# A decoder layer's mixer: one Gelu operation behind the attention's turned rows in place of a gelu in pieces

## The chip, the cores and the metric

The kernel runs on one core of a Trainium2 chip. The metric is the device time of one execution in microseconds. Five engines work side by side, each through its own instructions in order: TensorE (PE in the profile, its weight loads PEld), VectorE (DVE), ScalarE (ACT), GpSimd (POOL) and SyncE (SP), which issues most DMAs. They wait for each other on semaphores.

## The reference

One layer of a decoder trunk on 512 tokens of width 1024: a half-step SwiGLU FFN, a mixer, and a second half-step FFN, each with an RMS norm before and after it. The change lies in the mixer:

```python
proj = h @ w_in                       # split into x_lru, gate_lru, q, k, v
xc = causal_depthwise_conv(x_lru, conv_w, conv_b)
r, i = sigmoid(block_diag(xc, w_rg, b_rg)), sigmoid(block_diag(xc, w_ig, b_ig))
log_a = 8 * r * log_sigmoid(lam)
a, u = exp(log_a), sqrt(-expm1(2 * log_a)) * (i * xc)
h_t = a_t * h_(t-1) + u_t             # a scan over the tokens
y_lru = h * gelu(gate_lru)            # gelu in its tanh form
y_attn = sliding_window_sink_attention(q, k, v, sinks)
y = concat(rms_norm(y_lru, g_lru_out), rms_norm(y_attn, g_attn_out)) @ w_o
```

The recurrence has 512 channels, the attention 8 heads of 64 with a window of 128 tokens.

## The kernel before

Everything is float32, and a product is made of three TensorE products of split operands (`mm3`, L502 to L507: high by high, high by low, low by high), into one of eight PSUM banks of 128x512. The author writes the order of every engine by hand: the instructions stand in an engine's queue in the order in which the Python code makes them, and the framework adds the waits.

In the mixer the 512 channels are four chunks `ci` of 128 channels by 512 tokens. Before the attention loop, the convolution, the sigmoid gates, q, k and v are made. The attention loop (L1724 to L1755) runs over eight units `now`, a unit being a block `b` of 128 query tokens and one of two key heads `n`, plus two rounds to drain. In a round:

- `scores` (L1624): VectorE folds the two key blocks into one, takes the maximum and the exponent's offset; ahead of the first unit of a block TensorE makes the score products (L1622).
- `pump` (L1569): TensorE does some steps of the gate's product (`gt`, the four chunks of `gate_lru`), as filling.
- `turn_p` (L1661): TensorE turns the last unit's exponentials (`pt`, L1666), ScalarE copies them out (L1668), and POOL makes the two masked versions `pp` and `pa` (L1672, L1673).
- `exps` (L1651): ScalarE's exponentials of this unit (L1656).
- `run_due` (L1527): the steps set down for this round with `later`: pieces of the gelu, and the decay of the recurrence (`decay_a`, `decay_b`, L1574 to L1582).
- `values` (L1676): TensorE multiplies the masked exponentials of the unit before the last with the values (`po`, L1688 and L1689), VectorE divides (L1691 to L1696) into the row block `yn`; `b` below 2 lives in the tile `home`.

Beside this stand in the loop the roots of the recurrence (L1585, at `now == 5`, between two loads of ScalarE's function tables), `root_u` (L1588, at 6: chunks 0 and 1 on POOL, 2 and 3 on VectorE), and the scans (L1593: 2 and 3 at `now == 7`, 0 after the eighth unit, 1 after the loop). `W.fill` and `deferred` split the weights of the output product into high (ScalarE, L209) and low parts (VectorE, L185 and L214).

The gelu is in pieces. `gelu_a` scales the gate by the norm's factor (VectorE, L1427) and squares it (ScalarE, L536); `gelu_b` makes the cubic (VectorE, L1541); `gelu_c` takes the Tanh (ScalarE, L1544); `gelu_d` makes (1 + tanh) times gate (VectorE, L1548). Chunks 0 and 1 go through all of it in the loop, one piece a round. For chunks 2 and 3 the Tanh comes after the loop, and POOL and VectorE multiply the recurrence in two steps (L1797 with the gate, L1794 with 1 + tanh). POOL does the first multiplication of all four chunks. The factor of a half is left out, and the statistics' epsilon is four times as large (`eps4`, L1803).

After the loop `root_rms` and `invert_rms` (L1708, L1711) take the root of the mean squares of the row blocks `yns` and scale them: blocks 0 and 1 on ScalarE (L1715), 2 and 3 on VectorE (L1717). TensorE turns them (`atp`, L1770), ScalarE writes the high parts (`x_high`, L580), VectorE the low parts (`x_low`, L583), and the output product begins with the attention's half (`wo_attn`, L1813 and L1816). Then the recurrence's squares are summed (`add_square`, L1789 and L1791), TensorE makes the statistics (`rms_lru`, L550), VectorE scales the recurrence (L1833), and its half of the output product follows.

Of the kernel before, what the change touches and what calls it, by code (L numbers as in the profile page):

```python
# [11 lines left out]
AF = mybir.ActivationFunctionType  # L12
ALU = mybir.AluOpType
# [4 lines left out]
NB = T // P  # L18
# [5 lines left out]
KC = C // P  # L24
# [97 lines left out]
def tile_layer(ctx: ExitStack, tc: tile.TileContext, out: bass.AP, **ins: bass.AP):  # L122
    nc = tc.nc
    pe, dve, act, pool, sync = nc.tensor, nc.vector, nc.scalar, nc.gpsimd, nc.sync
# [11 lines left out]
    ALL = slice(0, T)  # L136
# [25 lines left out]
    def wt(name, w=T, dt=F32):  # L162
        return tmp.tile([P, w], dt, tag="w", name=name, bufs=NW)
# [311 lines left out]
    mean_c = filled("mean_c", 1, 1.0 / C)  # L475
    eps = filled("eps", 1, EPS)
    eps4 = filled("eps4", 1, 4 * EPS)
    dummy = const.tile([P, 1], F32, name="dummy")

    def preload(func):  # L480
        act.activation(dummy, eps, func)
# [52 lines left out]
    def square(src, sl, name, scale=1.0):  # L534
        sq = wt(f"sq_{name}")[:, sl]
        act.activation(sq, src, AF.Square, scale=scale)  # L536
        return sq
# [44 lines left out]
    def x_low(x, src, gain, sl):  # L582
        dve.scalar_tensor_tensor(x[1][:, sl], src, gain, x[0].bitcast(F32)[:, sl], op0=ALU.mult, op1=ALU.subtract)  # L583
# [612 lines left out]
    tps = turn_early()  # L1196
# [48 lines left out]
    tps = {c: turn(1, c) for c in range(0, KD, 2)}  # L1245
# [115 lines left out]
    for g, (f0, f1) in enumerate(GROUPS1):  # L1361
# [18 lines left out]
        for c in range(KD):  # L1380
# [25 lines left out]
            b = pair_banks[c] if c < 2 else product(W.take(), xs, name=f"ya{g}{c}")  # L1406
# [97 lines left out]
    for j in range(4):  # L1504
        b = in_product(f"pq{j}")
# [10 lines left out]
    preload(AF.Exp)  # L1516


    GC, GA = 0.7978845608028654, 0.044715
    Gs = {}  # L1520

    todo = []
# [1 line left out]
    def later(i, fn, *args):  # L1524
        todo.append((i, fn, args))

    def run_due(i):  # L1527
        nonlocal todo
        due, todo = [t for t in todo if t[0] <= i], [t for t in todo if t[0] > i]
        for _, fn, args in due:  # L1530
            fn(*args)


    gts, gqs = {}, {}

    def gelu_a(ci, b):
        gts[ci] = scaled(wt(f"gt{ci}"), b)
        gqs[ci] = square(gts[ci], ALL, f"g{ci}", (GC * GA) ** 0.5)

    def gelu_b(ci):  # L1540
        dve.scalar_tensor_tensor(gqs[ci], gqs[ci], GC, gts[ci], op0=ALU.add, op1=ALU.mult)  # L1541

    def gelu_c(ci):
        act.activation(gqs[ci], gqs[ci], AF.Tanh)  # L1544

    def gelu_d(ci):
        G = t2k(f"G{ci}")
        dve.scalar_tensor_tensor(G, gqs[ci], 1.0, gts[ci], op0=ALU.add, op1=ALU.mult)  # L1548
        Gs[ci] = G

    def fill_steps():
        for ci in range(KC):
            w = W.take(2)
            b = bank(f"gt{ci}")
            for k in range(KD):
                mm3(b, w, k, mx.xs[k], k == 0, k == KD - 1)
                if k < KD - 1:
                    yield
            if ci < KC - 1:
                for d, fn in enumerate((gelu_a, gelu_b, gelu_c, gelu_d)[:4 if ci < 2 else 1]):  # L1560
                    later(now + d, fn, *((ci, b) if d == 0 else (ci,)))
            else:
                gts[ci] = b
            yield

    now = 0
    steps = fill_steps()

    def pump(n):  # L1569
        for _ in range(n):  # L1570
            next(steps, None)


    def decay_a(ci):  # L1574
# [3 lines left out]
        m = gqs["m", ci] = wt(f"m{ci}")  # L1578
        act.activation(m, a, AF.Square)

    def decay_b(ci):
        dve.scalar_tensor_tensor(th[ci], gqs["m", ci], 1.0, th[ci], op0=ALU.add, op1=ALU.mult)  # L1582

    def root(ci):
        act.activation(th[ci], th[ci], AF.Sqrt)  # L1585

    def root_u(ci):
        (pool if ci < 2 else dve).tensor_mul(us_[ci], us_[ci], th[ci])  # L1588

    hl = us_  # L1590

    def scan(ci):
        dve.tensor_tensor_scan(hl[ci], rs_[ci], us_[ci], initial=0.0, op0=ALU.mult, op1=ALU.add)  # L1593


    scale = HD ** -0.5
    yns = []
# [108 lines left out]
    rat = const.tile([P, NB], F32, name="rat")  # L1706
# [3 lines left out]

    def invert_rms(bs):  # L1711
        dve.reciprocal(rat[:, bs], rat[:, bs])
        for b in range(NB)[bs]:
            if b < 2:
                act.activation(yns[b], yns[b], AF.Copy, scale=rat[:, b:b + 1])  # L1715
            else:
                dve.tensor_scalar(yns[b], yns[b], rat[:, b:b + 1], None, op0=ALU.mult)  # L1717

    units = [(b, n) for b in range(NB) for n in range(2)]
    for ci in range(KC):  # L1720
# [2 lines left out]
    n_units = len(units)  # L1723
    for now in range(n_units + 2):  # L1724
        if now < n_units:
            scores(*units[now])
            if now == 7:
                for ci in (2, 3):
                    scan(ci)
            if now in FILLS:  # L1730
                W.fill(FILLS[now])
        pump(PUMPS[now][0])
        if 0 <= now - 1 < n_units:
            turn_p(*units[now - 1])
        if now < n_units:
            exps(*units[now])
        if now == 0:
            deferred.run()
        if now <= n_units:
            run_due(now - 1)  # L1740
        pump(PUMPS[now][1])
        if 0 <= now - 2:
            values(*units[now - 2])
        if now == 5:
            for ci in range(KC):
                root(ci)
            preload(AF.Exp)
        if now == 6:
            for ci in range(KC):
                root_u(ci)  # L1750
        if now == n_units:
            scan(0)
            deferred.run()
            preload(AF.Sqrt)
            root_rms(slice(0, NB - 1))  # L1755


    root_rms(slice(NB - 1, NB))
    invert_rms(slice(0, NB - 1))
    invert_rms(slice(NB - 1, NB))  # L1760
    pump(100)
    ysp = [None] * KD
    scan(1)
    run_due(n_units + 1)
    gelu_b(KC - 2)
    gts[KC - 1] = scaled(wt(f"gt{KC - 1}"), gts[KC - 1])
    tps = [bank(f"atp{ci}") for ci in range(KC)]
    for ci, tp in enumerate(tps):
        for b in range(NB):
            pe.transpose(tp[:, b * P:(b + 1) * P], yns[b][:, ci * P:(ci + 1) * P], ident)  # L1770
        ysp[ci + KC] = (spare.pop(), spare.pop()) if spare else (t2k(f"yah{ci}", F32R), t2k(f"yal{ci}", F32R))
        x_high(ysp[ci + KC], tp, col("g_attn_out", ci), ALL)
        if ci == 2:
            gqs[KC - 1] = square(gts[KC - 1], ALL, f"g{KC - 1}", (GC * GA) ** 0.5)
            for i in (0, 1):
                x_low(ysp[i + KC], tps[i], col("g_attn_out", i), ALL)
            gelu_b(KC - 1)
            preload(AF.Exp)
    for ci in (2, 3):
        gelu_c(ci)  # L1780
    for ci in (2, 3):
        x_low(ysp[ci + KC], tps[ci], col("g_attn_out", ci), ALL)


    accl = tmp.tile([P, T], F32, tag="acc", name="acc_lru", bufs=3)
# [4 lines left out]
        else:  # L1790
            dve.tensor_add(accl, accl, square(hl[ci], ALL, f"l{ci}"))  # L1791

    def gated(ci):
        dve.scalar_tensor_tensor(hl[ci], gqs[ci], 1.0, hl[ci], op0=ALU.add, op1=ALU.mult)  # L1794

    for ci in (0, 2, 1, 3):
        pool.tensor_mul(hl[ci], hl[ci], Gs[ci] if ci in Gs else gts[ci])  # L1797
    for ci in (2, 3):
        gated(ci)
    for ci in range(KC):  # L1800
        add_square(ci)
    preload(AF.Sqrt)
    lrms = [InvRms([accl], mean_c, h, f"lru{h}", eps4) for h in range(2)]  # L1803

    res = Residual("r2", lambda c: col("mix_post_g", c))
    EARLY = KD - LATE
# [236 lines left out]
```

## Time and profile before

| | |
|---|---|
| time, three runs | 846.61, 846.87, 849.55 us; median 846.87 |
| the profiled execution | 846.56 us, its span 844.9 us |
| TensorE's granted clock | 0.998 |
| busy, of the span | TensorE 99%, VectorE 87%, ScalarE 62%, POOL 23% |
| convolution, gates, q, k, v | about 380 to 408 us |
| attention loop | about 408 to 456 us |
| turned rows, output product | from 457 us |

Times in a row of a timeline are the start from the beginning of the span and the length, both in us; then come engine, line of the kernel, operation, tiles written and read, shape and type, and a count of rows merged. Brackets at the end give idle time ahead of the row and what ended it. Rows of one engine overlap, since an engine begins the next operation before the last is done; what one operation holds of an engine is therefore read from start to start.

### The profile page before, as it was taken

To read this page: it belongs to the slowest core of one execution; us is meant where nothing else is said; L and a number is where in the kernel's file an instruction comes from. 1 tells how busy PE (TensorE), PEld (TensorE's weight loads), DVE (VectorE), ACT (ScalarE), POOL (GpSimd) and SP (SyncE) were. 2 spreads that over 40 slices of the span, in tenths; PEclk is the share of its full clock that TensorE was granted. 3 is DMA by queue.
4 is the path that set the end of the run, shared out by engine and by line. 5 is a ranking of instruction groups with operands and counts; after the bars stand their busy time and mean duration, and the time that the engine had idled before them with its cause. 6 is when DMAs were issued, how large, how long until landed. Compare 5 with 4: busy or idle time off the path is not lost.

```text
span 844.9 us, 12588 instructions
## 1 busy us (share of the span) xinstructions
PE 834.7 (99%) x4568; PEld 722.2 (85%) x4568; DVE 733.5 (87%) x1032; ACT 523.3 (62%) x842; POOL 196.2 (23%) x203
## 2 busy tenths in 40 slices
PE   9999999999999999999999999999999999999997
PEld 8988888988988998997787899888888888888886
DVE  4978999998979865889889679799998998998996
ACT  6646856666666654466787456436657767666562
POOL 2023000140320333334526055212004114032001
PEclk9999999999999999999999999999999999999999
DMA  7249419397595899222511131158539939769742
GB/s 251 77 130 347 157 54 319 85 248 255 133 249 180 172 274 331 71 89 84 161 43 50 50 101 51 50 118 269 194 118 225 314 96 251 259 144 252 306 145 100
DMA packets 123614, 143.74 MB, mean 170 GB/s; under 512 B 23896, under 2 KB 81568, under 8 KB 123040
## 3 DMA queue, kind: packets, MB, share of 16 engines
q1 hardware_dynamic: 109232, 111.86, 41.4%
q0 software_dynamic: 14176, 30.94, 17.0%
q8 instruction: 36, 0.59, 0.3%
q14 instruction: 26, 0.21, 0.1%
q10 hardware_dynamic: 144, 0.13, 0.0%
HBM read 100.45 MB, written 40.89 MB: 167 GB/s over the span
## 4 chain that ended last, share of the span: by engine, by line
PE 92%; DVE 4%; ACT 2%; issue 1%; DMA 1%; SPq 0%; DVEq 0%; ACTq 0%
PE aa L955 10%; PE ab L955 10%; PE da L955 5%; PE db L955 5%; PE yaa L1346 3%; PE bb L955 3%; PE ba L955 3%; PE yda L1346 2%; PE ya L506 2%; PE ya L505 2%; PE ya L507 2%; PE aa L885 1%; PE a_first L1205 1%; PE yab L1883 1%; PE yab L1884 1%; PE yab L1882 1%
## 5 line engine op out<-in xcount | busy, mean ns | idle before, releaser
L1115 POOL DMA_DIRECT2D yp_a<-stage x42 | 36.8, 1066 | 180.7 <-ACT stage L1112 163.5
L1115 POOL DMA_DIRECT2D yp_b<-stage x42 | 36.4, 1057 | 143.7 <-ACT stage L1112 121.4
L505 PE MATMUL ya<-hha,whi_ad 128*128 128x512 f32 x62 | 24.1, 389 | 0.0
L506 PE MATMUL ya<-hla,whi_ad 128*128 128x512 f32 x62 | 24.1, 389 | 0.0
L507 PE MATMUL ya<-hha,wlo_ad 128*128 128x512 f32 x62 | 24.1, 389 | 0.0
L688 POOL TENSOR_TENSOR acca_r<-acca_r,sq_r 128x512 f32<-128x512 f32 x6 | 8.1, 1358 | 51.9 <-ACT sq_r L536 51.9
L2001 POOL TENSOR_TENSOR last<-yp,grow 128x512 f32<-128x512 f32 x3 | 3.9, 1294 | 58.5 <-DVE yp L1991 58.5
L524 PE MATMUL an<-xh_mx,whi_xl 128*128 128x256 f32 x64 | 15.8, 287 | 0.0
L525 PE MATMUL an<-xh_mx,wlo_xl 128*128 128x256 f32 x64 | 15.5, 283 | 0.0
L1998 ACT ACTIVATE ysq<-yp 128x512 f32<-128x512 f32 (+1 forms) x8 | 4.8, 606 | 16.2 <-DVE yp L1991 16.2
L505 PE MATMUL gt<-xh_mx,whi_gt 128*128 128x512 f32 x32 | 14.2, 444 | 0.0
L507 PEld LDWEIGHTS ya<-hha,wlo_ad 128*128 128x128 f32 x62 | 11.6, 188 | 2.4
L505 PEld LDWEIGHTS ya<-hha,whi_ad 128*128 128x128 f32 x62 | 11.6, 188 | 2.4
L506 PEld LDWEIGHTS ya<-hla,whi_ad 128*128 128x128 f32 x62 | 11.6, 188 | 2.4
L1112 ACT COPY stage<-yab 128x512 f32<-128x512 f32 x12 | 6.5, 605 | 10.9 <-DMA yp_b<-stage 7.3
L536 ACT ACTIVATE sq_r<-yp_a 128x256 f32<-128x256 f32 (+1 forms) x10 | 5.0, 503 | 12.9 <-DVE yp_a L678 5.9
L505 PE MATMUL pq<-xh_mx,whi_q 128*128 128x512 f32 x32 | 12.8, 400 | 0.0
L505 PE MATMUL pub<-xh_f,whi_bu 128*128 128x512 f32 x32 | 12.6, 395 | 0.0
L507 PE MATMUL gt<-xh_mx,wlo_gt 128*128 128x512 f32 x32 | 12.6, 394 | 0.0
L505 PE MATMUL pgb<-xh_f,whi_bg 128*128 128x512 f32 x32 | 12.6, 393 | 0.0
L506 PE MATMUL gt<-xl_mx,whi_gt 128*128 128x512 f32 x32 | 12.6, 392 | 0.0
L506 PE MATMUL pq<-xl_mx,whi_q 128*128 128x512 f32 x32 | 12.5, 390 | 0.0
(2022 smaller groups left out, 3520.3 us busy)
## 6 DMA issues: line engine op xcount, KB each, us to landing
yp_a<-stage POOLq DMA_DIRECT2D x50, 256.0 KB, 8.8
yp_b<-stage POOLq DMA_DIRECT2D x50, 256.0 KB, 9.4
h_a<-za SPq DMA_DIRECT2D x16, 256.0 KB
hxa<-h_a SPq DMA_DIRECT2D x16, 256.0 KB
h_b<-zb SPq DMA_DIRECT2D x16, 256.0 KB
hxb<-h_b SPq DMA_DIRECT2D x16, 256.0 KB
xn<-in_x SPq DMA_DIRECT2D x8, 256.0 KB
xT_hbm<-xT POOLq DMA_DIRECT2D x2, 1024.0 KB, 9.3
```

Of the source, the lines that this page charges most:

```text
L505: pe.matmul(ps, hi[:, k, :], xh, start=start, stop=False)
L506: pe.matmul(ps, hi[:, k, :], xl, start=False, stop=False)
L507: pe.matmul(ps, lo[:, k, :], xh, start=False, stop=stop)
L524: pe.matmul(ps[:, sl], hi[:, k, :], xh, start=k == 0, stop=False)
L525: pe.matmul(ps[:, sl], lo[:, k, :], xh, start=False, stop=False)
L885: pe.matmul(o, w[:, k, js], x, start=first and i + j + k == 0, stop=k == 3 and i == 2, skip_group_check=True)
L955: pe.matmul(b[tb], x[:, blk], w[:, k, :], start=first and q + k + j == 0, stop=q + k == 2 and j == 2, skip_group_check=True)
L1115: pool.dma_start(o, st.rearrange("p (a b) -> p a b", a=2) if len(o.shape) == 3 else st, accum_op=ALU.add)
L1205: pe.matmul(banks[j][:, HALF[0]], ws[j][part][:, k, :], n1.xs[k][xpart][:, HALF[0]], start=k == 0 and part == xpart, stop=stop and k == KD ...
L1346: pe.matmul(o, a[:, k, ms], x[:, js], start=first and i + k + m % 2 == 0, stop=k == 1 and i == 2, skip_group_check=True)
L1882: pe.matmul(banks[i], hh[:, js], hi[:, k, :], start=first and k == 0, stop=False, skip_group_check=True)
L1883: pe.matmul(banks[i], hh[:, js], lo[:, k, :], start=False, stop=False, skip_group_check=True)
```

## The change

The gelu becomes one ScalarE operation, `Gelu_apprx_tanh`, over the scaled gate, in place. All four chunks of the gate are only scaled in the loop (chunk 3 after it), into tiles of their own. The four Gelus stand on ScalarE behind the four high parts of the turned rows, after a load of their table. The squares, the cubics, the Tanhs, the last products and `eps4` go. VectorE makes all products of the recurrence: all four `root_u`, chunks 0 and 1 one round later than before, and after the low parts the four products with the Gelu. POOL keeps only the masks there. The normalised rows are scaled in another order: in the last round of the loop, ahead of its `values`, the reciprocal of blocks 0 to 2 is taken and ScalarE scales block 0; after the loop VectorE scales blocks 2, 1 and then 3. Scan 1 stands behind the scaling of gate 3.

```diff
-    def gelu_a(ci, b):
-        gts[ci] = scaled(wt(f"gt{ci}"), b)
-        gqs[ci] = square(gts[ci], ALL, f"g{ci}", (GC * GA) ** 0.5)
...
-    def gelu_d(ci):
-        G = t2k(f"G{ci}")
-        dve.scalar_tensor_tensor(G, gqs[ci], 1.0, gts[ci], op0=ALU.add, op1=ALU.mult)
-        Gs[ci] = G
+    def turned_gate(ci, b):
+        Gs[ci] = scaled(t2k(f"G{ci}"), b)
+
+    def gelu(ci):
+        act.activation(Gs[ci], Gs[ci], AF.Gelu_apprx_tanh)
...
-            if ci < KC - 1:
-                for d, fn in enumerate((gelu_a, gelu_b, gelu_c, gelu_d)[:4 if ci < 2 else 1]):
-                    later(now + d, fn, *((ci, b) if d == 0 else (ci,)))
-            else:
-                gts[ci] = b
+            later(now, turned_gate, ci, b)
...
     def root_u(ci):
-        (pool if ci < 2 else dve).tensor_mul(us_[ci], us_[ci], th[ci])
+        dve.tensor_mul(us_[ci], us_[ci], th[ci])
...
     def invert_rms(bs):
         dve.reciprocal(rat[:, bs], rat[:, bs])
-        for b in range(NB)[bs]:
-            if b < 2:
-                act.activation(yns[b], yns[b], AF.Copy, scale=rat[:, b:b + 1])
-            else:
-                dve.tensor_scalar(yns[b], yns[b], rat[:, b:b + 1], None, op0=ALU.mult)
+
+    def scale_rows(b):
+        if b == 0:
+            act.activation(yns[b], yns[b], AF.Copy, scale=rat[:, b:b + 1])
+        else:
+            dve.tensor_scalar(yns[b], yns[b], rat[:, b:b + 1], None, op0=ALU.mult)
...
+        if now > n_units:
+            invert_rms(slice(0, NB - 1))
+            scale_rows(0)
         if 0 <= now - 2:
             values(*units[now - 2])
...
         if now == 6:
-            for ci in range(KC):
+            for ci in (2, 3):
+                root_u(ci)
+        if now == 7:
+            for ci in (0, 1):
                 root_u(ci)
...
     root_rms(slice(NB - 1, NB))
-    invert_rms(slice(0, NB - 1))
+    for b in (2, 1):
+        scale_rows(b)
     invert_rms(slice(NB - 1, NB))
+    scale_rows(NB - 1)
     pump(100)
     ysp = [None] * KD
+    run_due(n_units + 1)
     scan(1)
-    run_due(n_units + 1)
-    gelu_b(KC - 2)
-    gts[KC - 1] = scaled(wt(f"gt{KC - 1}"), gts[KC - 1])
...
         x_high(ysp[ci + KC], tp, col("g_attn_out", ci), ALL)
...
-    for ci in (2, 3):
-        gelu_c(ci)
-    for ci in (2, 3):
+    preload(AF.Gelu_apprx_tanh)
+    for ci in range(KC):
+        gelu(ci)
+    for ci in range(KC):
         x_low(ysp[ci + KC], tps[ci], col("g_attn_out", ci), ALL)
...
-    for ci in (0, 2, 1, 3):
-        pool.tensor_mul(hl[ci], hl[ci], Gs[ci] if ci in Gs else gts[ci])
-    for ci in (2, 3):
-        gated(ci)
+    for ci in range(KC):
+        dve.tensor_mul(hl[ci], hl[ci], Gs[ci])
...
-    lrms = [InvRms([accl], mean_c, h, f"lru{h}", eps4) for h in range(2)]
+    lrms = [InvRms([accl], mean_c, h, f"lru{h}") for h in range(2)]
```

More of the change, by code (lines that the diff above doesn't have):

```diff
@@ L1516, in tile_layer @@
     preload(AF.Exp)
-    GC, GA = 0.7978845608028654, 0.044715
     Gs = {}
@@ L1531, in run_due @@
             fn(*args)
-    gts, gqs = {}, {}
-    def gelu_a(ci, b):
-        gts[ci] = scaled(wt(f"gt{ci}"), b)
-        gqs[ci] = square(gts[ci], ALL, f"g{ci}", (GC * GA) ** 0.5)
[L1540 to L1544, printed above, removed]
-    def gelu_d(ci):
-        G = t2k(f"G{ci}")
-        dve.scalar_tensor_tensor(G, gqs[ci], 1.0, gts[ci], op0=ALU.add, op1=ALU.mult)
-        Gs[ci] = G
+    def turned_gate(ci, b):
+        Gs[ci] = scaled(t2k(f"G{ci}"), b)
+    def gelu(ci):
+        act.activation(Gs[ci], Gs[ci], AF.Gelu_apprx_tanh)
     def fill_steps():
@@ L1571, in pump @@
             next(steps, None)
+    squares = {}
     def decay_a(ci):
@@ L1577, in decay_a @@
         act.activation(a, a, AF.Exp, scale=ka[:, ci:ci + 1])
-        m = gqs["m", ci] = wt(f"m{ci}")
+        m = squares[ci] = wt(f"m{ci}")
         act.activation(m, a, AF.Square)
     def decay_b(ci):
-        dve.scalar_tensor_tensor(th[ci], gqs["m", ci], 1.0, th[ci], op0=ALU.add, op1=ALU.mult)
+        dve.scalar_tensor_tensor(th[ci], squares[ci], 1.0, th[ci], op0=ALU.add, op1=ALU.mult)
     def root(ci):
@@ L1772, in tile_layer @@
         x_high(ysp[ci + KC], tp, col("g_attn_out", ci), ALL)
[L1773 to L1778, printed above, removed]
-    for ci in (2, 3):
-        gelu_c(ci)
-    for ci in (2, 3):
+    preload(AF.Gelu_apprx_tanh)
+    for ci in range(KC):
+        gelu(ci)
+    for ci in range(KC):
         x_low(ysp[ci + KC], tps[ci], col("g_attn_out", ci), ALL)
@@ L1791, in add_square @@
             dve.tensor_add(accl, accl, square(hl[ci], ALL, f"l{ci}"))
-    def gated(ci):
-        dve.scalar_tensor_tensor(hl[ci], gqs[ci], 1.0, hl[ci], op0=ALU.add, op1=ALU.mult)
-    for ci in (0, 2, 1, 3):
-        pool.tensor_mul(hl[ci], hl[ci], Gs[ci] if ci in Gs else gts[ci])
-    for ci in (2, 3):
-        gated(ci)
+    for ci in range(KC):
+        dve.tensor_mul(hl[ci], hl[ci], Gs[ci])
     for ci in range(KC):
```

## The prediction

> **What bounds the kernel now.** I read the page first, then the chain of work that ended last, the waits of TensorE, and last the timelines of each engine from 425 to 470 us. From the page come the span, the busy times and the chain by engine:
>
> ```profile
> span 844.9 us, 12588 instructions
> ...
> PE 834.7 (99%) x4568; PEld 722.2 (85%) x4568; DVE 733.5 (87%) x1032; ACT 523.3 (62%) x842; POOL 196.2 (23%) x203
> ...
> PE 92%; DVE 4%; ACT 2%; issue 1%; DMA 1%; SPq 0%; DVEq 0%; ACTq 0%
> ```
>
> TensorE is the bound, and the built program of the changed kernel gives it the same 4329 rows in the same order. So the change can pay only where TensorE now stands still, and cost only where it newly waits. TensorE's timeline (start, us, line, tiles) shows where it stands in the attention loop. A row that waits for its weights is drawn long, so I go from start to start:
>
> ```profile
> 435.75 0.38 PE L1622 MATMUL sc<-kTh,qT2h 64*128 64x256 f32 x1 [0.16 <-ACT sc L1656]
> ...
> 441.98 0.39 PE L506 MATMUL gt<-xl_mx,whi_gt 128*128 128x512 f32 x1
> 442.21 0.40 PE L507 MATMUL gt<-xh_mx,wlo_gt 128*128 128x512 f32 x1
> 442.64 1.10 PE L1666 MATMUL pt<-ident,sc 128*128 128x128 f32 x4
> 443.50 0.48 PE L505 MATMUL gt<-xh_mx,whi_gt 128*128 128x512 f32 x1
> ...
> 446.77 0.60 PE L1666 MATMUL pt<-ident,sc 128*128 128x128 f32 x4
> 447.12 0.48 PE L505 MATMUL gt<-xh_mx,whi_gt 128*128 128x512 f32 x1
> ...
> 447.68 0.40 PE L507 MATMUL gt<-xh_mx,wlo_gt 128*128 128x512 f32 x1
> 448.29 0.44 PE L1688 MATMUL po<-home,pp 128*128 128x65 f32 x2 [0.22 <-POOL pp L1672]
> 449.80 0.44 PE L1689 MATMUL po<-home,pa 128*128 128x65 f32 x2 [1.07 <-POOL pa L1673]
> ...
> 451.38 0.48 PE L505 MATMUL gt<-xh_mx,whi_gt 128*128 128x512 f32 x1
> ...
> 452.16 0.33 PE L1688 MATMUL po<-home,pp 128*128 128x65 f32 x2
> ...
> 453.86 0.48 PE L505 MATMUL gt<-xh_mx,whi_gt 128*128 128x512 f32 x1
> ```
>
> Four turns of a unit take 0.35 (446.77 to 447.12), a full block of 16 value products 1.70 (452.16 to 453.86), and a gate product 0.23 (441.98 to 442.21). So TensorE loses 0.16 at 435.75; 442.64 − 442.21 − 0.23 = 0.20 and 0.86 − 0.35 = 0.51 at the turns; 448.29 − 447.68 − 0.23 = 0.38 and 451.38 − 448.29 − 1.70 = 1.39 at the values of the block. Together 2.64 us. The chain says who is behind it (start, us):
>
> ```profile
> 442.04 1.64 DVE xc L1588 x2
> ...
> 445.50 1.18 DVE es L1648
> ...
> 449.31 0.97 DVE sq_g L1541
> ...
> 456.67 1.24 ACT home L1715 x2
> ...
> 468.02 0.85 PE rms_lru L550 x8
> ```
>
> From 442 to 456 VectorE carries the end, then two ScalarE scalings, then TensorE without a break up to the statistics at 468.
>
> **The change part by part.**
>
> *The gelu's pieces leave the attention loop.* ScalarE loses a Tanh that stands in front of the Sqrt table, and VectorE a cubic step ahead of a unit's scores:
>
> ```profile
> 435.07 1.14 ACT L1656 ACTIVATE sc<-sc,nm 128x128 f32<-128x128 f32 x4 [1.52 <-DVE nm L1645]
> ...
> 436.18 0.65 ACT L1544 ACTIVATE sq_g<-sq_g 128x512 f32<-128x512 f32 x1
> ```
>
> ```profile
> 431.08 1.12 DVE L1541 SCALAR_TENSOR_TENSOR sq_g<-sq_g,gt 128x512 f32<-128x512 f32 x1
> 432.12 0.15 DVE L1691 TENSOR_TENSOR rden<-po,es 128x4 f32<-128x4 f32 x1
> ```
>
> The step holds VectorE 432.12 − 431.08 = 1.04, and the exponentials at 435.07 wait for VectorE; they come 1.04 earlier, and the next ones, behind the Tanh, 1.04 + 0.65 = 1.7. The stalls of 0.16, 0.20 and 0.51 hang on these exponentials and are smaller: all go. −0.87.
>
> *POOL's two root products go to VectorE, one round later.*
>
> ```profile
> 444.14 2.52 POOL L1588 TENSOR_TENSOR xc<-xc,th 128x512 f32<-128x512 f32 x2
> 446.61 1.63 POOL L1672 TENSOR_SCALAR_AFFINE_SELECT pp<-pa 128x512 f32<-128x512 f32 x1
> 448.31 1.44 POOL L1673 TENSOR_SCALAR_AFFINE_SELECT pa<-pa 128x512 f32<-128x512 f32 x1
> ```
>
> The two masks that TensorE awaits at 448.29 and 449.80 stand behind these products. Without them, and with the turns 0.87 earlier, both are made before TensorE arrives, even if they still take 1.63 and 1.44. −0.38 − 1.39. TensorE would then reach the turning of the normalised rows, 2.64 earlier than now.
>
> *What is late next: the scaled rows.* The turning waits for the last scaling of row block 3 on VectorE:
>
> ```profile
> 456.70 0.16 DVE L1712 RECIPROCAL rat<-rat 128x1 f32<-128x1 f32 x1 [0.50 <-ACT rat L1709]
> 456.90 0.73 DVE L1717 TENSOR_SCALAR yn<-yn,rat 128x512 f32<-128x512 f32 x1
> ```
>
> ```profile
> 458.12 0.38 PE L1770 MATMUL atp<-ident,yn 128*128 128x128 f32 x2
> ```
>
> VectorE's queue up to 456.90 changes by these terms. Its two root products took 1.64 with POOL at work beside them; the lone row is 0.68 long and such rows start 0.6 apart (464.16 below), so 1.2 with the masks over earlier: −0.4. The 8-column sum at 445.50 took 1.18 and ended with POOL's second product (444.14 + 2.52 = 446.66); the 4-column sum at 432.12 takes 0.15: −1.0. The cubic step at 449.31: −0.97. The wait of 0.50 at 456.70: −0.5, since another scaling fills it. Scores earlier by TensorE's first stall: −0.16. Added are two root products, 2 × 0.6 = +1.2, and that scaling of a block which ScalarE had, 0.55 as an estimate below the 0.73 of its like: +0.55. Sum −1.3; small waits for TensorE's values inside, which I leave out, make it rather −1.5, and I take −1.4. The scaling ends at 457.63 − 1.4 = 456.2. TensorE's turn of row block 3, the second of the pair at 458.12, so 458.23, comes at 456.2: −2.0. TensorE is ready sooner, so VectorE decides, and of the 2.64 some is lost again while TensorE waits here.
>
> *Behind the turned rows: Gelu, products, sums of squares.* Rows of before, ScalarE and then VectorE:
>
> ```profile
> 458.54 0.69 ACT L580 ACTIVATE attn<-atp,cols 128x512 fp32r<-128x512 f32 x1 [0.64 <-PE atp L1770]
> ...
> 461.30 1.28 ACT L481 ACT_TABLE_LOAD   x1
> 462.59 0.20 ACT L481 ACTIVATE dummy<-eps 128x1 f32<-128x1 f32 x1
> ...
> 463.27 1.14 ACT L1544 ACTIVATE sq_g<-sq_g 128x512 f32<-128x512 f32 x2
> ...
> 464.84 1.67 ACT L536 ACTIVATE sq_l<-xc 128x512 f32<-128x512 f32 x3
> ```
>
> ```profile
> 457.56 1.21 DVE L1593 TENSOR_TENSOR_SCAN xc<-r,xc 128x512 f32<-128x512 f32 x1
> ...
> 462.84 1.40 DVE L583 SCALAR_TENSOR_TENSOR yal<-atp,cols,yah 128x512 fp32r<-128x512 f32 x2
> 464.16 1.28 DVE L1794 SCALAR_TENSOR_TENSOR xc<-sq_g,xc 128x512 f32<-128x512 f32 x2
> ...
> 465.49 2.28 DVE L1791 TENSOR_TENSOR acc_lru<-acc_lru,sq_l 128x512 f32<-128x512 f32 x3
> ```
>
> The sum of squares ends at 465.49 + 2.28 = 467.77, and the chain has TensorE at the statistics at 468.02: no slack, so this tail must move as much as the turns. After the change ScalarE copies the four turned blocks from 458.54 − 2.0 = 456.55, 0.6 apart, to 458.95; table and dummy bring 460.35. No row shows a Gelu. The nearest is the Tanh pair, 1.14 for two, so 0.54 apart; at worst it is the scaled copy, 0.69, without overlap. It is one operation of the same shape, so less than the Tanh is excluded; I take 0.54, and the fourth ends at 462.6. VectorE meanwhile does gate 3's scaling, the scan and four low parts (456.2 + 0.65 + 1.2 + 2.7 = 460.75), waits for the first Gelu, 460.95, and multiplies 0.6 apart. ScalarE's squares start at 462.5, the second ends at 463.65, and the three sums take 2.28: 465.95. Against 467.77 that is −1.8, so TensorE (−2.0) waits 0.2 there. POOL's four gate products are gone with that; VectorE's four, in their place, are in the sum above.
>
> New waits and what stands behind them: gate 3's scaling waits on VectorE for the last gate product, with scan 1 and the low parts behind it, but the turns end later than that product; the first multiplication waits for the first Gelu, with all sums and so TensorE's statistics behind it, as counted. At nothing I cost the epsilon of the last statistics (another constant, the same row) and the DMAs: SP's 175 rows stand in the same order, and no transfer is added or moved past another.
>
> **Sum:** −1.8 us, all in the mixer; what follows hangs on the statistics and moves with it. The profiled execution took 846.56 around its span of 844.9, so 844.8; the median of the runs shown, 846.87, lies 0.3 above it, and from it I get 845.1, my forecast. Bounds: Gelu at 0.69 makes the tail 4 × 0.15 = 0.6 later, 845.7; VectorE's two slow rows kept, +1.4 less what the wait of 0.2 hides, 846.3; all of 2.64 kept and 0.5 more at the turning, 843.8.
>
> A rule on the table load speaks against the change. In the rows the dummy at 462.59 starts 0.01 behind the load's end. The Trainium skill, "ScalarE: Activation LUTs", section "What ACT_TABLE_LOAD costs", adds a drain of some 1.38 to each switch. By the page the tail would end about 1.4 later, which is the first rival's size; the load above shows none, so the sum keeps 1.28.
>
> **The rivals.** *The tail eats the gain.* TensorE comes 2.0 early to the statistics and waits, since table, Gelus, products and squares now stand in one line behind the turns. If that line is 1.4 longer, 0.4 is left: 846.5. For it: no slack before. Against: four operations of 0.6 are not enough. *VectorE stays slow.* Two more products ahead of scan 0, and 1.64 and 1.18 kept: 846.3. *Gelu is dear: slower than before.* Each 0.1 on one Gelu costs the tail 0.4. From 0.54 + 1.8 / 4 = 1.0 apart the kernel is slower; at 1.24, a Tanh and a second pass, the tail is 2.8 later: +1.0, 847.9. To lose 4.2 us (0.5%, about what a measurement of this kernel can tell from no change) takes 2.0 apart. *The work that left was hidden:* 846.9; the bracketed waits above speak against it.
>
> **How the numbers follow.** Forecast 0.62, slow VectorE 0.12, tail 0.12, hidden 0.04, dear Gelu 0.08, more gain than any stall shown 0.02. The range, 843.8 to 847.0, leaves out the dear Gelu and the last. Faster by over 4.2 us is more than the stalls of this stretch hold: 0.02. Slower by over 4.2 is the worse part of the dear Gelu: 0.04. Within: 0.94.
>
> **What would show it.** In the changed profile: no stall at the turns now at 442.64 or the values now at 448.29; the turning of row block 3 right behind VectorE's last scaling, at about 456; Gelus 0.54 apart; a wait of 0.2 at the statistics. Wrong would be Gelus over 0.8 apart, a wait over 1 us at the statistics, masks still late, or a new stall at the last block of values.

## The result, and the profile after

The changed kernel takes 844.52 us (median of 8 executions, 843.99 to 845.10) against 846.73 (846.46 to 849.55) for the kernel before beside it: a ratio of 0.997, 95% interval 0.9959 to 0.9981. The forecast was 845.1. The profiled execution took 844.61 us around a span of 842.9. In all that follows, before was run 97 times and after 17 times, and their spreads differ: 845.8 to 851.0 for before, 844.0 to 845.1 for after. That turned out to be a second effect of the change, which no step of the prediction held (below).

The page of the changed kernel, the lines that answer to the first fence of the prediction:

```profile
span 842.9 us, 12574 instructions
...
PE 834.0 (99%) x4568; PEld 722.1 (86%) x4568; DVE 729.9 (87%) x1031; ACT 520.7 (62%) x837; POOL 184.6 (22%) x197
...
PE 93%; DVE 3%; ACT 2%; DMA 1%; issue 0%; POOL 0%; DVEq 0%; POOLq 0%; ACTq 0%
```

POOL has 11.6 us less to do, and TensorE 0.7. Shares of a whole span say little about a change of 2 us; the timelines around it do. TensorE of the changed kernel (start, length, line, tiles; idle time and its releaser in brackets):

```profile
441.63 0.60 PE L1652 MATMUL pt<-ident,sc 128*128 128x128 f32 x4
...
445.25 1.09 PE L1652 MATMUL pt<-ident,sc 128*128 128x128 f32 x4
...
446.87 0.33 PE L1674 MATMUL po<-home,pp 128*128 128x65 f32 x2
...
454.58 0.55 PE L1763 MATMUL atp<-ident,home 128*128 128x128 f32 x2
...
455.88 0.33 PE L1763 MATMUL atp<-ident,yn 128*128 128x128 f32 x1 [0.64 <-DVE yn L1704]
...
465.68 1.05 PE L550 MATMUL rms_lru<-mean_c,acc_lru 128*128 128x1 f32 x8
```

Row against row, the same instruction stands here and there. Where the loop is entered, after is 0.29 earlier already: the input arrived sooner in this execution, which has nothing to do with the change, and I take it off. A second profile of the changed kernel (844.72 us) enters the loop when before does. The turns drawn at 442.64 come at 441.63, those at 446.77 at 445.25 with a new stall of 0.5 (the row is 1.09 long, not 0.60). The values that waited at 448.29 and 449.80 follow at 446.87 without a break. Row block 3 is turned at 455.88 and not at 458.23: −2.35, or −2.06 without the head start. The statistics stand at 465.68 and not at 467.86: −1.89. The second profile has these two at 456.18 and 465.99: −2.05 and −1.87 without anything to take off.

VectorE of the changed kernel:

```profile
441.21 1.56 DVE L1574 TENSOR_TENSOR xc<-xc,th 128x512 f32<-128x512 f32 x2
...
444.75 0.17 DVE L1634 TENSOR_TENSOR es<-nm,sinks 128x8 f32<-128x8 f32 x1
...
447.81 1.75 DVE L1574 TENSOR_TENSOR xc<-xc,th 128x512 f32<-128x512 f32 x2
...
451.96 1.20 DVE L185 TENSOR_TENSOR wlo_wo<-raw_wo__4325,whi_wo 128x1024 fp32r<-128x1024 f32 x1
...
455.34 0.49 DVE L1704 TENSOR_SCALAR yn<-yn,rat 128x512 f32<-128x512 f32 x1
...
460.74 2.50 DVE L1782 TENSOR_TENSOR xc<-xc,G 128x512 f32<-128x512 f32 x4 [0.57 <-ACT G L1537]
463.35 2.28 DVE L1779 TENSOR_TENSOR acc_lru<-acc_lru,sq_l 128x512 f32<-128x512 f32 x3
```

The last scaling ends at 455.83, and TensorE, idle for 0.64, starts on it 0.05 later: VectorE's queue decides here. The sums end at 465.63, and the statistics start 0.05 later: the tail decides there. ScalarE of the changed kernel, between the two:

```profile
458.69 1.28 ACT L481 ACT_TABLE_LOAD   x1
459.98 0.20 ACT L481 ACTIVATE dummy<-eps 128x1 f32<-128x1 f32 x1
460.09 2.18 ACT L1537 ACTIVATE G<-G 128x512 f32<-128x512 f32 x4
462.18 0.61 ACT L1777 ACTIVATE acc_lru<-xc 128x512 f32<-128x512 f32 x1
462.70 1.66 ACT L536 ACTIVATE sq_l<-xc 128x512 f32<-128x512 f32 x3
```

The four Gelus take 462.18 − 460.09 = 2.09, so 0.52 apart, and the dummy starts 0.01 behind the table load's end. In this execution a little is given back far behind the mixer. From TensorE's waits in the changed kernel (engine, line, what it waited for: us in total, times, longest):

```profile
PE ab L955 <- ACT bb L960: 0.3, 1, 0.3
```

This stands at 596.34, where ScalarE's copy of a bank is behind two casts. The same product stands at 598.31 before, so the gain is 1.68 behind it. The second profile has no such wait: the product stands at 596.44, the gain there is still 1.87, and the span is 843.0 against 844.9. So the 0.2 belong to one execution and not to the change.

### The profile page after: what moved, and what is told of

Its sections match the earlier page's. It is cut to its first block, busy times and chain, and to the rows that moved or that the text cites. A ratio compares the mean times of both kernels' runs of the same rounds, so it can differ in the third digit from the quotient of the medians.

```text
span 842.9 us, 12574 instructions
## 1 busy us (share of the span) xinstructions
PE 834.0 (99%) x4568; PEld 722.1 (86%) x4568; DVE 729.9 (87%) x1031; ACT 520.7 (62%) x837; POOL 184.6 (22%) x197
## 4 chain that ended last, share of the span: by engine, by line
PE 93%; DVE 3%; ACT 2%; DMA 1%; issue 0%; POOL 0%; DVEq 0%; POOLq 0%; ACTq 0%
PE ab L955 10%; PE aa L955 10%; PE da L955 5%; PE db L955 5%; PE yaa L1346 3%; PE bb L955 3%; PE ba L955 3%; PE yda L1346 2%; PE ya L505 2%; PE ya L506 2%; PE ya L507 2%; PE a_first L1205 1%; PE aa L885 1%; PE yab L1867 1%; PE yab L1866 1%; PE yab L1865 1%
## 5 line engine op out<-in xcount | busy, mean ns | idle before, releaser
L507 PEld LDWEIGHTS ya<-hha,wlo_ad 128*128 128x128 f32 x62 | 11.6, 188 | 2.4
L505 PEld LDWEIGHTS ya<-hha,whi_ad 128*128 128x128 f32 x62 | 11.6, 188 | 2.4
L506 PEld LDWEIGHTS ya<-hla,whi_ad 128*128 128x128 f32 x62 | 11.6, 188 | 2.4
```

The source lines that it names most:

```text
L505: pe.matmul(ps, hi[:, k, :], xh, start=start, stop=False)
L506: pe.matmul(ps, hi[:, k, :], xl, start=False, stop=False)
L507: pe.matmul(ps, lo[:, k, :], xh, start=False, stop=stop)
```

## The experiments

Theory: TensorE's stalls in the loop went with the gelu's pieces and POOL's products; VectorE's queue up to the last scaling, and then the line from the turned rows to the statistics, set what is left. Rivals: one part of the change does it alone, VectorE's queue doesn't decide, the tail has slack. All kernels were timed beside the kernel before, whose executions in the three groups had medians of 846.72, 846.81 and 848.81 (29, 34 and 26 executions).

**Only the root products moved** (in the kernel before; gelu in pieces and scaling as they were):

```diff
     def root_u(ci):
-        (pool if ci < 2 else dve).tensor_mul(us_[ci], us_[ci], th[ci])
+        dve.tensor_mul(us_[ci], us_[ci], th[ci])
...
         if now == 6:
-            for ci in range(KC):
+            for ci in (2, 3):
+                root_u(ci)
+        if now == 7:
+            for ci in (0, 1):
                 root_u(ci)
```

> The kernel before with one part of the change alone: VectorE makes all four root products, chunks 0 and 1 one round later; the gelu stays in pieces. Theory (VectorE's queue up to the scaling of row block 3 sets the turning of the rows): the stall of 1.4 + 0.4 us at the values of the sixth unit goes, but VectorE gets 1.2 more and saves only some 1.0 to 1.4, so the rows are scaled when they were and TensorE waits at the turning instead: within 0.4 us of before, 846.7. Rival (the masks behind POOL's products were what cost): 1.7 us less than before, 845.0.

Measured: 847.34 (846.76 to 847.87, 12 executions), by the medians 0.6 above the kernel before beside it: neither the theory's 0.4 nor the rival's 845.0. TensorE of this kernel:

```profile
449.20 0.44 PE L1689 MATMUL po<-home,pa 128*128 128x65 f32 x2 [0.59 <-POOL pa L1673]
...
458.19 0.33 PE L1773 MATMUL atp<-ident,home 128*128 128x128 f32 x1 [1.23 <-ACT home L1715]
458.80 0.33 PE L1773 MATMUL atp<-ident,home 128*128 128x128 f32 x1 [0.28 <-ACT home L1715]
```

The wait for `pa` is 0.59 here and 1.07 before. But it is 0.58 in another kernel whose instructions up to there are those of before ("The same on the kernel before", below), so it differs from one execution to the next, and these rows don't show that the moved products shortened it. At the turning TensorE waits 1.23 + 0.28, behind VectorE's longer queue, where before it waits 0.28. Alone, this part gains nothing. But its 12 executions lie within 1.1 us, those of before beside it within 4.8.

**The root products back on POOL** (in the changed kernel, all four at round 6 as before):

```diff
     def root_u(ci):
-        dve.tensor_mul(us_[ci], us_[ci], th[ci])
+        (pool if ci < 2 else dve).tensor_mul(us_[ci], us_[ci], th[ci])
```

> The changed kernel with one part undone: POOL makes the root products of chunks 0 and 1 in the round in which it did before. Theory (VectorE's queue sets the end of the loop): the masks come later, yet TensorE, which waits 0.8 us for the scaled rows in the changed kernel, has room for it, and VectorE has 1.2 less to do: as fast as the changed kernel or up to 0.6 faster, 843.9 to 844.5. Rival (late masks cost what they cost before): the stall of 1.7 us is back at the values of the sixth unit, 845.7 or more.

Measured: the profiled execution took 844.25, as the theory has it; but the 12 executions lie between 844.25 and 852.22, median 846.22. The same kernel again:

> The kernel with POOL's two root products, one more time: its profiled execution was as fast as the changed kernel's (844.25 us against 844.61), but the median of its 12 executions was 846.2 and they lay between 844.3 and 852.2. Theory A, the scatter came with that stretch of time on the chip and not with the kernel: median 844.0 to 844.8 now, and a spread below 1.5 us. Theory B, the products on two engines at once make the kernel itself scatter: median above 845.5 and a spread above 4 us again.

Measured: median 846.03, 844.06 to 852.57: the kernel scatters, and it was no matter of the hour (theory B). This time the profile caught a long execution, 850.19. VectorE, POOL and TensorE of the first execution (844.25), one fence each:

```profile
441.15 2.66 DVE L1574 TENSOR_TENSOR xc<-xc,th 128x512 f32<-128x512 f32 x2
```

```profile
441.55 3.40 POOL L1574 TENSOR_TENSOR xc<-xc,th 128x512 f32<-128x512 f32 x2
```

```profile
446.12 1.10 PE L1652 MATMUL pt<-ident,sc 128*128 128x128 f32 x4 [0.78 <-ACT sc L1642]
```

And of the second (850.19):

```profile
441.59 3.42 DVE L1574 TENSOR_TENSOR xc<-xc,th 128x512 f32<-128x512 f32 x2
```

```profile
441.50 2.96 POOL L1574 TENSOR_TENSOR xc<-xc,th 128x512 f32<-128x512 f32 x2
```

```profile
447.32 1.10 PE L1652 MATMUL pt<-ident,sc 128*128 128x128 f32 x4 [1.54 <-ACT sc L1642]
```

VectorE's pair takes 1.56 in the changed kernel, where one of POOL's masks (441.00 to 441.64) stands beside its beginning, and 2.66 or 3.42 with POOL's pair beside it. With nothing beside it, in the profile of "Each Gelu twice" below, it takes 1.28 (from 441.39). In the first execution VectorE started first (441.15 against 441.55), in the second POOL (441.50 against 441.59), and each time the first had the shorter time. The Trainium skill, "GPSIMD Engine Reference", section "Specifications", says that POOL's interfaces to SBUF are shared with VectorE, with contention when a VectorE operation has two SBUF inputs; these rows agree, and give it a price of 1.4 to 2.1 us on a pair of 128x512 products. The 0.76 that VectorE lost went into TensorE's wait, 1.54 instead of 0.78. Then this, in the stretches of the 850.19 execution (length, busy time of each engine with the number of instructions, and behind POOL the granted TensorE clock, DMA share, GB/s):

```profile
core 0: us, PE busy (x) PEld busy (x) DVE busy (x) ACT busy (x) POOL busy (x), PEclk, DMA share, GB/s
444.00:449.00 5.00, 3.46 (x21) 2.49 (x20) 4.86 (x9) 1.73 (x6) 2.14 (x3) 1.00 0.00 0
449.00:454.00 5.00, 5.00 (x23) 4.71 (x22) 3.02 (x9) 2.50 (x6) 1.27 (x2) 0.51 0.00 0
454.00:459.00 5.00, 5.00 (x20) 4.56 (x20) 3.15 (x8) 1.72 (x4) 0.00 (x0) 0.50 0.44 146
459.00:464.00 5.00, 5.00 (x31) 4.34 (x30) 2.95 (x5) 1.89 (x5) 0.00 (x0) 0.97 0.18 64
```

After the stall TensorE's clock is halved for some 10 us although it is busy all the while. That is 5 us of lost work, and 850.19 less 5 is what executions of this kernel without a fall take (11 of the 24, at a mean clock of 0.998 or above: 844.06 to 845.60). Their median is 845.40 and only two lie in the theory's 843.9 to 844.5, so even without a fall POOL's products cost some 0.9 here; but neither profile has a wait for a mask, which was the rival's reason. The Trainium skill, "TensorE: Matmul & The Clock Gate", section "Part 1: The HAM clock gate", knows the two states, half and full, and names at least one idle window of some 3.4 us as the way down. The two states agree; the length doesn't: here an idle stretch of 1.54 was enough, and the measurement decides.

**Only the gelu** (the changed kernel with POOL's root products, as above, and the old scaling, as below):

> Only the gelu is changed against the kernel before: POOL keeps its two root products, and the rows are scaled in the old order. Theory, with the cubic steps and the Tanhs out of the loop POOL's products start 1.2 us sooner or more and are over before the masks are due, so the gelu's part alone brings the gain, less the 0.5 that the old scaling order costs: 844.4 to 845.2. Rival, the masks are freed by the moved products, as the prediction counts it (0.38 + 1.39): 846.0 or above.

Measured: median 846.57, 845.02 to 852.33. Neither number was right, for the same reason: six of 12 executions, at a clock of 0.998 or above, take 845.02 to 845.74, the theory's upper end and a little over it; the other six, 847.4 to 852.3, lost clock. These are all of TensorE's waits in its profile (what it waited for: us in total, times, longest):

```profile
PE pt L1652 <- ACT sc L1642: 1.5, 1, 1.5
PE warm L1192 <- POOL ident masks.py:199: 1.4, 1, 1.4
PE ab L955 <- ACT bb L960: 0.4, 1, 0.4
PE yeb L1862 <- DVE hls L838: 0.3, 1, 0.3
PE xtp L1139 <- DMA xn<-in_x: 0.3, 1, 0.3
PE a_first L1205 <- ACT xh_a L580: 0.3, 1, 0.3
```

No mask (`po`) is among them, with POOL's products still there. So the masks were freed by the gelu, and not by the moved products; what POOL's products cost now stands at the turns (`pt`).

**The old scaling** (the changed kernel, rows scaled behind the loop as before):

```diff
-        if b == 0:
+        if b < 2:
             act.activation(yns[b], yns[b], AF.Copy, scale=rat[:, b:b + 1])
...
-        if now > n_units:
-            invert_rms(slice(0, NB - 1))
-            scale_rows(0)
...
-    for b in (2, 1):
+    invert_rms(slice(0, NB - 1))
+    for b in range(NB - 1):
         scale_rows(b)
```

> The changed kernel with one part undone: all scaling of rows behind the loop, blocks 0 and 1 on ScalarE, 2 and 3 on VectorE, as before. Theory: block 1 is ready on ScalarE only at about 456.3 in place of block 3 at 455.9, so TensorE's turning comes 0.4 to 0.7 later: 844.9 to 845.2. Rival (the order of the scaling does nothing, since VectorE's last row decides either way): 844.5.

Measured: 845.07 (844.14 to 845.33), as the theory has it: beside the moved root products this part is worth 0.5. TensorE then waits for two scalings in a row on ScalarE:

```profile
455.30 0.33 PE L1761 MATMUL atp<-ident,home 128*128 128x128 f32 x1 [0.95 <-ACT home L1702]
455.92 0.33 PE L1761 MATMUL atp<-ident,home 128*128 128x128 f32 x1 [0.29 <-ACT home L1702]
```

Where the gelu is one operation, four kernels now tell the other two parts apart. Medians of the executions at a mean clock of 0.998 or above, with their number; the kernel before has 846.57 (62):

| root products | old scaling | new scaling |
|---|---|---|
| on POOL | 845.18 (6) | 845.40 (11) |
| on VectorE | 845.00 (11) | 844.50 (17) |

The gelu's part alone is worth 1.4 of the 2.1. The moved products and the new scaling bring the rest only together: each alone changes the median by 0.2, one of them upwards.

**VectorE's queue shortened** (the changed kernel; the low part of a weight, 1.20 at 451.96, moved behind the sums, and the products of a last lone column in the order high parts, then low parts):

```diff
             scan(0)
-            deferred.run()
             preload(AF.Sqrt)
...
     for ci in range(KC):
         add_square(ci)
+    deferred.run()
     preload(AF.Sqrt)
...
-        for k in ks:
-            for c in cs:
-                for part in ws[c]:
+        if len(cs) == 1:
+            c, = cs
+            for part in ws[c]:
+                for k in ks:
...
```

> The changed kernel with the one deferred low part of the output weights (1.2 us on VectorE, between scan 0 and the last divisions) moved behind the sums of squares; TensorE's passes for that column take all high parts first, so that the low part is in time. Theory (VectorE's queue ahead of the scaled rows is what is late): the rows are scaled 0.8 to 1.1 us earlier, TensorE turns them without a wait, and the tail, which begins at the turns, moves too: 0.6 to 0.8 less than the changed kernel, 843.8. Rival (the tail of Gelu, products and sums is bound by itself and does not move): TensorE waits at the statistics, 844.5.

> The run with the late low part once more, since it had 6 executions so far. Theory: median 843.0 to 843.6, none above 845, 1.1 to 1.3 us under the changed kernel's on the same chip. Rival, the difference was the draw: within 0.4 of the changed kernel.

Measured: 843.27 (842.60 to 844.64) and 843.69 (843.13 to 844.15), six executions each, against 844.49 for the changed kernel beside the second. So −1.2 (844.52 less 843.27), more than the 0.7 expected, and −0.8 the second time, 0.3 less than then expected and just outside the 843.0 to 843.6; ratio to before in the first group 0.9957 (0.9941 to 0.9973). It is the fastest version of this study. The whole stretch, in the columns of the table of stretches above (busy time of TensorE first):

```profile
436.00:465.00 29.00, 29.00 (x176) 25.16 (x177) 24.41 (x50) 22.47 (x47) 3.81 (x6) 1.00 0.00 1
```

No wait is left at the turning (row block 3 at 454.59 against 455.88), and the tail moved with it (statistics 464.33 against 465.68). That VectorE's queue set this place is shown.

**The same on the kernel before**, with the same edit:

> The kernel before, with the deferred low part of a weight moved off VectorE's queue ahead of the row scaling, as in the run with the late low part, and nothing else. Theory, before the change TensorE's own stalls (2.64 us) had it at the turning 0.7 us ahead of the scaled row block 3, so only 0.5 to 0.7 of the 1.2 on VectorE can be had: 845.9 to 846.3. Rival, VectorE's queue alone decided: 845.5. Rival, its squares and sums don't come sooner: 846.7.

Measured: median 846.11; nine executions between 845.64 and 846.57 and three at 849.1 to 850.1. The median is as the theory has it, but its profile doesn't show the theory's reason:

```profile
448.25 0.44 PE L1689 MATMUL po<-home,pa 128*128 128x65 f32 x2 [0.58 <-POOL pa L1673]
...
456.24 0.33 PE L1769 MATMUL atp<-ident,home 128*128 128x128 f32 x1 [0.17 <-ACT home L1715]
456.85 0.33 PE L1769 MATMUL atp<-ident,home 128*128 128x128 f32 x1 [0.28 <-ACT home L1715]
```

At the turning TensorE waits for ScalarE's two scalings, as it does before, and not for VectorE's. And at the masks it stands 0.80 from start to start (449.84 − 447.34 − 1.70), against 0.38 + 1.39 before, though the instructions up to there are the same. How much of the 0.7 below the median of before (846.81) comes from VectorE's queue is therefore open.

**Each Gelu twice, and two Gelus twice** (the changed kernel with extra work):

```diff
     def gelu(ci):
+        act.activation(wt(f"again{ci}"), Gs[ci], AF.Gelu_apprx_tanh)
         act.activation(Gs[ci], Gs[ci], AF.Gelu_apprx_tanh)
```

> Extra work that the reference doesn't have: each of the four Gelus is issued once more, into a scratch tile, ahead of the one that counts. Theory, table, Gelus, products and sums stand in one line behind the turned rows and have no slack: 4 times 0.52 us longer, of which TensorE's wait at the statistics shows all, that wait grows from 0.15 to about 2.2 us and the time from 844.5 to 846.6. Rival, the tail has slack: 844.5, wait at the statistics below 0.5.

> Extra work that the reference doesn't have: two of the four Gelus, those of blocks 0 and 1, are issued once more into a scratch tile. Theory, the line from the turned rows to the statistics has no slack: 2 times 0.52 us more, so a wait of 1.0 to 1.3 us at the statistics, too short to lower the clock: 845.4 to 845.8 and a spread below 2 us. Rival, the 4.6 us that all four cost come from something other than their length: below 845.0 or above 846.5.

Measured: 849.13 (848.00 to 850.31), and with two 847.28 (845.50 to 848.07). The statistics in the one with four, then in the one with two:

```profile
468.10 1.26 PE L550 MATMUL rms_lru<-mean_c,acc_lru 128*128 128x1 f32 x8 [2.62 <-DVE acc_lru L1780]
```

```profile
467.10 1.05 PE L550 MATMUL rms_lru<-mean_c,acc_lru 128*128 128x1 f32 x8 [1.31 <-DVE acc_lru L1781]
```

The eight take 0.59 apart and not 0.52, so four more cost 2.6. Two more make the wait 1.31, as the theory says, and four 2.62 where 2.2 was foretold: the tail has no slack. The times are higher than foretold, by the clock again, so the theory's "too short to lower the clock" is wrong; the stretches of the one with two, in the same columns:

```profile
464.00:468.00 4.00, 2.69 (x16) 2.03 (x16) 2.65 (x4) 3.52 (x7) 0.00 (x0) 1.00 0.00 0
468.00:472.00 4.00, 4.00 (x13) 3.19 (x13) 3.45 (x6) 2.15 (x4) 0.00 (x0) 0.57 0.00 0
472.00:476.00 4.00, 4.00 (x19) 3.35 (x18) 2.12 (x5) 0.72 (x1) 0.00 (x0) 1.00 0.75 248
```

After 1.31 us of waiting the clock is halved for most of the next 4 us: 4 × 0.43 = 1.7. Three of the 12 executions had no fall, and took 845.50 to 845.86, the theory's 845.4 to 845.8; nine had one, 847.0 to 848.1. With four Gelus twice all 12 had one: 844.5 + 2.6 + some 2.

**A stall without POOL** (the changed kernel with two more products on VectorE):

```diff
             for ci in (2, 3):
                 root_u(ci)
+            for i in range(2):
+                dve.tensor_mul(wt(f"fill{i}"), us_[3], th[3])
```

> The changed kernel with extra work that the reference doesn't have: two more 128x512 products on VectorE behind its first two root products, into scratch tiles, 2 times 0.75 us, with nothing beside them on POOL. They make TensorE's wait at the next turns, 0.5 us in the changed kernel, 1.9 to 2.0 us long. Theory, a stall of about 1.5 us or more takes TensorE's clock to 0.50 for some 10 us after it, whatever caused it: executions of 847.5 to 853 in at least a third of 12, mean clock 0.992 to 0.997 in these. Rival, it is POOL's products beside VectorE's that make executions differ: all of them between 845.4 and 846.6, clock 0.998, 1.5 us over the changed kernel for the longer queue on VectorE.

Measured: median 846.71, 845.41 to 851.76. In the profiled execution, 845.83:

```profile
446.95 1.10 PE L1652 MATMUL pt<-ident,sc 128*128 128x128 f32 x4 [1.45 <-ACT sc L1642]
```

From start to start the stall is 2.1 long (from 445.34, the end of the gate's last product, to 447.81, the start of its next, less the 0.35 of four turns), a little more than the 1.9 to 2.0 foretold; 1.45 of it is drawn as idle, the rest in the row. Two of POOL's masks stood beside the added products (443.47 and 444.17), so it was not quite nothing. The clock did not fall in this execution. Two others took 849.73 and 851.76 at a mean clock of 0.991 to 0.992. Three more, 846.7 to 847.0 at 0.997, can't be told from those at 0.999, which reach 846.75; the profile of "The old scaling" has a mean of 0.997 as well, with the full clock up to 839, where TensorE's products are over. So it is fewer than the theory's third, but not the rival's 845.4 to 846.6: the added products, which are all that differs from the changed kernel, bring long executions without any product on POOL, though two in 12 against none in 17 is a small number, and neither of them was profiled.

**The changed kernel once more**:

> The changed kernel once more, beside the kernel before on the same chip. Theory, its longest TensorE stall is below 0.7 us, so its clock never falls: 844.0 to 845.2 in every one of 12 executions, while about 3 in 10 executions of the kernel before lie above 848.5. Rival, the 8 executions so far were a lucky draw: at least one above 847.

Measured: 844.49 (844.00 to 844.84, nine executions), while 14 of the 26 executions of before in this group took over 848.5, at a mean clock of 0.993 or 0.994. The theory's 3 in 10 was too low for this hour, its other half holds.

## Why the prediction was right, and where it was not

The forecast's sum held: −1.8 in the mixer, measured −1.89 and in the second profile −1.87. Its mechanism held in outline: TensorE's stalls go, VectorE's queue decides next, and then the tail. That the sum came out so close is partly luck, since terms of it were wrong both ways. By its steps:

- **Stalls at the exponentials, −0.87.** All three went, and they were larger than read: TensorE was 1.23 ahead at the turns now at 445.25. The first stall was read off the bracket as 0.16. From the start of the scores to the next gate product (two rows of before, then two of after) it is 2.15 − 1.63 = 0.52:

```profile
434.50 0.39 PE L1622 MATMUL sc<-kTh,qT0h 64*128 64x256 f32 x2
...
436.65 0.50 PE L505 MATMUL gt<-xh_mx,whi_gt 128*128 128x512 f32 x1
```

```profile
434.20 0.39 PE L1608 MATMUL sc<-kTh,qT0h 64*128 64x256 f32 x2
...
435.83 0.50 PE L505 MATMUL gt<-xh_mx,whi_gt 128*128 128x512 f32 x1
```

  Then the new stall of 0.5 took some back, and TensorE was 0.75 ahead when it came to the values. The prediction named only the last block's values as a place for a new stall.
- **Masks, −0.38 − 1.39.** The whole 1.77 went, but for another reason than I gave. I hung it on the moved products. With only these moved, TensorE still stood 0.80 at the values (0.59 of it in the bracket) and 1.5 at the turning; with only the gelu changed, the masks were in time behind POOL's own products. The gelu's cubic steps and Tanhs had held up everything in front of them.
- **The turning waits for VectorE's last scaling.** In before it did not. That scaling ended at 457.63, and its block was turned at 458.23, 0.6 later; what TensorE waited for there was ScalarE's second scaling:

```profile
457.95 0.33 PE L1770 MATMUL atp<-ident,home 128*128 128x128 f32 x1 [0.28 <-ACT home L1715]
```

  So the −2.0 at the turning holds two things: VectorE's queue, 1.4, and 0.6 behind it, which goes only because ScalarE's second scaling is taken away. The prediction has no words for the second. Undoing the new scaling cost 0.5.
- **VectorE's queue, −1.4.** The last scaling ended at 455.83 against 457.63, −1.5 without the head start, by errors that cancel. The products' gain of 0.4 was 0.1 (1.56, with a mask of POOL's beside the pair; without it 1.28, near the 1.2 foretold), the two added took 1.7 and not 1.2; the es sum went from 1.18 to 0.17 as said; the scalings take 0.49 and not 0.73, and the added one holds VectorE 0.40 and not 0.55.
- **VectorE decides, then the tail.** TensorE's waits of 0.64 and about 0.15 (0.2 foretold) stand where they were put, and shortening the queue and lengthening the tail both moved the end.
- **Gelu at 0.54 apart.** 0.52, a little under the Tanh's 0.54, which the prediction had excluded. Of the drain that the Trainium skill ("ScalarE: Activation LUTs", "What ACT_TABLE_LOAD costs") adds to a load, the new load shows nothing: 458.69 + 1.28 = 459.97, and the dummy starts at 459.98.
- **What follows moves with it.** It does: the 0.2 lost at 596 in one profile are not lost in the other.

The step that failed is one under all sums: that a stall costs its own length. The rivals were priced so. The first gave 1.4 for a tail 1.4 longer; two Gelus twice made the tail 1.2 longer and cost 2.8 in the median (847.28 against 844.49). The dear Gelu, 1.24 apart, was to be 2.8 over the forecast; with each done twice, 1.19 apart, it was 4.6 over the changed kernel. The difference is the halved clock. For the forecast it did no harm, since the changed kernel's longest drawn wait there is 0.64. But it means that the change did more than the forecast says. Of the 89 executions of before beside the experiments, 27 had a mean clock of 0.992 to 0.994 and took 848.6 to 851.0; the other 62, at 0.998 or above, had a median of 846.57. After had no such execution in 17. By means, 847.6 against 844.5, the gain is 3.2; by the medians of the forecast's comparison it is 2.2. How many executions of before fall differs by group (5 of 29, 8 of 34, 14 of 26), so the 3.2 is no fixed number.

What stays open: no execution of before with a lower clock was profiled, so that the fall there comes behind its stall at the masks is argued from its POOL products and from the kernels above, not shown. What decides whether a stall brings a fall is open too, and its length alone doesn't: waits of 1.23 and 0.28 behind one another ("Only the root products moved") brought no long execution in 12, one of 1.31 at the statistics brought one in 9 of 12. Not tried was ScalarE's copy at 596 moved ahead of the casts.

## What to carry to other kernels

Ask what held up the first late instruction of a queue before moving the one next to the stall: here a cubic step and a Tanh ahead of the scores freed masks on a third engine, and the products between them didn't have to move for that. Keep TensorE's single stalls short. Here the kernels whose longest wait inside the work was drawn 0.64 (the changed one) and 0.95 (the old scaling) had no long execution in 17 and 12; a longer one can cost several times its length, and then the median and the spread of a kernel differ by more than its sum of durations tells. Two engines that read pairs of tiles side by side make each other's time uncertain, and what waits for them inherits that.

## What the hardware did that I had not expected

- **The clock falls after a short stall.** Drawn idle of 0.64, 0.78, 0.95, 1.07 and 1.23 was followed by no fall in the executions profiled; 1.31, 1.51, 1.54 and 2.62 were; 1.45 was not in one. Read in stretches of 1 us, the clock stood at 0.50 for 3.4 us after each of the two stalls at the statistics, and for 10.2 and 13.7 us after the two at the turns (850.19 and 852.33 us): close to 1, 1, 3 and 4 times 3.4. Half of that is the time lost: 852.33 less 6.8 is 845.5, inside the 845.02 to 845.74 of that kernel's executions without a fall.
- **Products on VectorE and POOL at once.** The pair on VectorE took 1.28 alone, 2.66 and 3.42 with POOL's beside it; POOL's pair 2.96 to 3.40, and 2.52 before, where VectorE had no product of that size beside it. Whichever started first had the shorter time.
